# Attention with a bias: one VectorE product over four score banks instead of two, E tiles of twelve banks, AV lag of four slots

## The chip, the cores and the metric

The kernel runs on one core of a Trainium2 chip. The metric is the device time of one execution in microseconds (us), as a median over runs. The profiles give a "span", which is about 2 us shorter than the time of the same run. All runs compared here are of the fast state; one early run of the kernel before took 303.93 us and is left out. Ratios are the mean time of one kernel's runs over that of the other's in the same rounds, so they are not quite the ratio of the medians quoted.

Engine names in the profile lines: PE is TensorE (PEld its weight loads), DVE is VectorE, ACT is ScalarE, POOL is GpSimd. "L120" is line 120 of that kernel's source; the same statement has another line number in another version, so lines are named by what they do.

## The reference

Inputs are q, k and v of shape 4 x 8 x 1024 x 64 (32 heads) and one bias of 1024 x 1024 shared by all heads.

```python
scores = scale * np.matmul(q, k.transpose(0, 1, 3, 2)) + bias
attn = np.exp(scores - max) / (sum of exp + 1e-8)
out = np.matmul(attn, v)
```

The kernel uses exp(s + bias) = exp(s) * exp(bias). It keeps exp(bias^T) in bf16 as `eb`, computes E = exp(scale * k q^T) on ScalarE and multiplies E by `eb` on VectorE. A column of ones appended to v makes the AV product ("attention times v") deliver the sums of the softmax too.

## The kernel before

The heads are taken in 16 pairs. A score bank is 128 keys x 512 queries, and the program walks through 512 of them. Each slot makes three banks on TensorE into one of only two score buffers and one exponential on ScalarE reads them:

```python
ps_s = ctx.enter_context(tc.tile_pool(name="ps_s", bufs=2, space=bass.MemoryType.PSUM))  # 2 x 3 banks
ps_x = ctx.enter_context(tc.tile_pool(name="ps_x", bufs=1, space=bass.MemoryType.PSUM))  # tags xa, xb: 1 bank each
...
def s_slot(g):
    ps = ps_s.tile([P, 3, HQ], F32, tag="s", name="ps")
    ...  # three matmuls, kT x qT
    nc.scalar.activation(e[:, o:o + n, :], ps[:, :n, :], ACTF.Exp, scale=scale)

def mul_pair(b):                       # VectorE, two banks (both heads of a key chunk share eb)
    ...
    nc.vector.tensor_tensor(e[:, o:o + 2, :], e[:, o:o + 2, :],
                            eb[:, qh, kc, :].unsqueeze(1).to_broadcast([P, 2, HQ]), op=ALU.mult)
```

Two uses share the bank "xa": the AV accumulator `po` of the first head, and the result `px` of transposing the next q or k. VectorE must empty either before TensorE may write the other:

```python
def transpose_pe(pr, which):
    px = ps_x.tile([P, NCH, P], BF, tag="xb" if pr < 2 and which else "xa", name="px")
    ...  # 16 transposes on TensorE
    def copy():                        # VectorE: masked copy to qT (q) or plain copy to kT (k)
        ...
    return copy

def av_bank(b):
    if kc == 0:
        po[h] = ps_x.tile([P, QC, D1], F32, tag="xa" if h == 0 else "xb", name="po")
    ...  # 4 matmuls; after the eighth bank it returns evac(), VectorE's normalisation
```

Each step of the main loop puts one slot in program order. In the traces VectorE's instructions come in that order, and one that waits holds up those behind it (below, a copy starts at 64.95 us behind a product that waited until 64.34):

```python
for step, item in enumerate(order):
    ...  # scores and exponential of this slot; in 28 steps a transpose of q or k
    ...  # up to four AV banks whose product is at least LAG = 3 steps old
    muls(1)              # a product of two banks, of exponentials up to the slot before
    for f in late:       # the copy of a transpose, and evacuations
        f()
    muls(2)
    exp_b = new_b
```

The softmax here doesn't subtract the row's maximum and nothing guards it: scores larger than these inputs give would overflow.

## Time and profile before

The median before is 266.6 us (11 runs, 265.5 to 267.5).

| reading | value | view |
|---|---|---|
| ScalarE busy | 91% of the span | page, busy times |
| VectorE, TensorE busy | 86%, 84% | page, busy times |
| pitch of exponentials, back to back | about 1.35 us | ScalarE's timeline |
| stops of ScalarE from 52 us to the end | 5.8 us in 13 stops | ScalarE's timeline |
| last exponential's end to the end of the span | 6.4 us | ScalarE's timeline |

Busy times of the page (us, share of the span, instructions), and two of its groups: the exponential, and the product. A group's columns are busy time and mean ns of one, then the engine's idle time before them and what ended most of it.

```profile
PE 221.0 (84%) x3136; PEld 137.6 (52%) x3136; DVE 227.2 (86%) x422; ACT 240.7 (91%) x179; POOL 52.5 (20%) x72
...
L120 ACT ACTIVATE E<-ps 128x1536 bf16<-128x1536 f32 x171 | 232.4, 1475 | 16.7 <-PE ps L113 14.6
L136 DVE TENSOR_TENSOR E<-E,eb 128x1024 bf16<-128x1024 bf16 x256 | 167.1, 687 | 18.9 <-ACT E L120 14.1
```

ScalarE is nearly full. VectorE waits for it directly; ScalarE waits for VectorE only through TensorE, as shown below. One exponential lasts 1.475 us, but the next starts before it ends, which is why the pitch is shorter. The Trainium skill ("ScalarE: Activation LUTs", What ACT_TABLE_LOAD costs) gives 186 ns plus 0.833 ns an element for an activation with immediate scale and bias, as here (the kernel gives a number for the scale and no bias). That makes an estimate of 1466 ns; the trace agrees (1475 ns).

ScalarE's own timeline (start, length, what, count; in brackets the idle time before) shows how little room is left:

```profile
51.98 15.01 ACT L120 ACTIVATE E<-ps 128x1536 bf16<-128x1536 f32 x11 [0.32 <-PE ps L113]
67.48 14.88 ACT L120 ACTIVATE E<-ps 128x1536 bf16<-128x1536 f32 x11 [0.48 <-ACT E L120]
82.92 13.60 ACT L120 ACTIVATE E<-ps 128x1536 bf16<-128x1536 f32 x10 [0.56 <-PE ps L113]
96.84 15.02 ACT L120 ACTIVATE E<-ps 128x1536 bf16<-128x1536 f32 x11 [0.32 <-PE ps L113]
```

Three stops return every 44.86 us, in which three head pairs (32 slots) pass. The Trainium skill ("Perfetto Trace Analysis", Optimization Strategy) says that a gap that repeats on the engine that should be saturated can mean too little SBUF or PSUM for the next tile. Here it fits in part: the stop of 0.48 us comes from the single bank "xa". The timeline of that stop, with weight loads left out:

```profile
62.85 4.14 ACT L120 ACTIVATE E<-ps 128x1536 bf16<-128x1536 f32 x3
...
63.76 0.64 PE L86 MATMUL px<-ident,qr 128*64 128x128 bf16 x16
...
64.34 0.69 DVE L136 TENSOR_TENSOR E<-E,eb 128x1024 bf16<-128x1024 bf16 x1 [0.24 <-ACT E L120]
64.46 0.81 PE L113 MATMUL ps<-qT,kT 128*128 128x512 bf16 x3
64.95 1.22 DVE L92 TENSOR_TENSOR qT<-px,mask 128x2048 bf16<-128x2048 bf16 x1
...
66.22 0.53 PE L150 MATMUL po<-vall,E 128*128 128x65 bf16 x12 [0.83 <-DVE qT L92]
66.58 0.81 PE L113 MATMUL ps<-qT,kT 128*128 128x512 bf16 x3
...
67.48 1.45 ACT L120 ACTIVATE E<-ps 128x1536 bf16<-128x1536 f32 x1 [0.48 <-ACT E L120]
```

Read it as a chain. TensorE transposes q into "xa". VectorE has a product before the copy in its order; the product waits for an exponential until 64.34, and so the copy qT runs from 64.95 to 66.17. TensorE needs "xa" for AV, stands 0.83 us, and makes the next scores only at 66.58. ScalarE starts at 67.48 instead of 67.00. The two score buffers hide only a part of such a stand: in one period TensorE's stands behind q copies of 0.71, 0.83 and 0.95 us became stops of 0.32, 0.48 and 0.56 us, and its stands behind k copies (0.42, 0.30 and 0.17 us) became none. About 0.4 us is hidden. The bracket of this last line names ScalarE itself as the releaser; it is put down to the last event that the profile saw, and the scores that end just before are the better reading.

Who waited for whom over the whole run (us in total, times, longest):

```profile
PE po L150 <- DVE qT L92: 10.9, 14, 1.0
...
PE po L150 <- DVE kT L97: 4.3, 14, 0.4
```

### The profile page before, as it was taken

Reading aid. Unit: us, or ns where it says so; the run is one execution under the profiler, and the core shown is the slowest. Engines: PE = TensorE matmul, PEld = TensorE weight load, DVE = VectorE, ACT = ScalarE, POOL = GpSimd, SP = SyncE. Lnnn points to the kernel's source line nnn. Section 1 sums busy time; section 2 is a strip of 40 time slices with the busy share of each in tenths; the row PEclk is TensorE's granted clock in tenths of the full one; section 3 lists DMA queues with packets and bytes.
Section 4 is the critical chain, followed back from the end, with each engine's and each line's share of the span. In section 5 each row is a group of like instructions: output and inputs, shape, how many; then the busy total and the mean of one; then the engine's idle time right before and its main releaser. Section 6 shows DMA issues by size and latency. Waiting matters only on the chain.

```text
span 264.5 us, 7204 instructions
## 1 busy us (share of the span) xinstructions
PE 221.0 (84%) x3136; PEld 137.6 (52%) x3136; DVE 227.2 (86%) x422; ACT 240.7 (91%) x179; POOL 52.5 (20%) x72
## 2 busy tenths in 40 slices
PE   1577879888998989899898989899898989899883
PEld 1244545555655555555555555555555555555552
DVE  4246679998999999899899899989999998998984
ACT  2289999999999999999999999999999999999990
POOL 8353004022130404031040404022091000000000
PEclk9999999999999999999999999999999999999999
DMA  6999904919191673929194684919089201111112
GB/s 89 176 217 185 170 1 94 108 46 157 43 148 14 119 81 77 126 51 151 40 122 43 106 94 98 102 42 161 17 150 118 82 0 42 42 40 42 40 43 79
DMA packets 46912, 23.53 MB, mean 89 GB/s; under 512 B 34337, under 2 KB 42529, under 8 KB 46625
## 3 DMA queue, kind: packets, MB, share of 16 engines
q0 software_dynamic: 42272, 14.68, 51.8%
q1 hardware_dynamic: 4608, 8.39, 8.7%
q8 instruction: 24, 0.39, 0.6%
q14 instruction: 8, 0.06, 0.1%
HBM read 29.36 MB, written 8.39 MB: 143 GB/s over the span
## 4 chain that ended last, share of the span: by engine, by line
ACT 44%; DVE 26%; PE 18%; DMA 4%; issue 4%; POOL 2%; ACTq 0%; POOLq 0%
ACT E L120 42%; DVE E L136 16%; PE ps L113 13%; DVE qT L92 5%; PE po L150 5%; DMA qr<-in_q_dram 4%; DVE kT L97 3%; ACT eb L130 2%; DVE oall L161 2%; DVE rs L160 1%; POOL vall L76 1%; POOL kr L70 1%; ACTq L120 0%; POOL qr L71 0%; PE px L86 0%
## 5 line engine op out<-in xcount | busy, mean ns | idle before, releaser
L120 ACT ACTIVATE E<-ps 128x1536 bf16<-128x1536 f32 x171 | 232.4, 1475 | 16.7 <-PE ps L113 14.6
L136 DVE TENSOR_TENSOR E<-E,eb 128x1024 bf16<-128x1024 bf16 x256 | 167.1, 687 | 18.9 <-ACT E L120 14.1
L113 PE MATMUL ps<-qT,kT 128*128 128x512 bf16 x512 | 139.7, 382 | 14.5 <-ACT E L120 10.9
L150 PEld LDWEIGHTS <-E 128*128 128x128 bf16 x2048 | 84.2, 98 | 54.6 <-issue 19.5
L150 PE MATMUL po<-vall,E 128*128 128x65 bf16 x2048 | 94.1, 194 | 16.1 <-DVE qT L92 10.9
L113 PEld LDWEIGHTS <-kT 128*128 128x128 bf16 x512 | 44.2, 98 | 45.1 <-issue 20.7
L70 POOL DMA_DIRECT2D kr<-in_k_dram x16 | 11.3, 708 | 139.7 <-PE px L86 86.0
L161 DVE TENSOR_TENSOR oall<-po,rs 128x256 f32<-128x256 f32 x64 | 27.2, 425 | 2.2
L76 POOL DMA_DIRECT2D vall<-in_v_dram x32 | 28.1, 883 | 0.0
L92 DVE TENSOR_TENSOR qT<-px,mask 128x2048 bf16<-128x2048 bf16 x16 | 19.5, 1219 | 2.5 <-PE px L86 2.3
L97 DVE COPY kT<-px 128x1024 bf16<-128x1024 bf16 x16 | 11.0, 685 | 7.5 <-PE px L86 7.5
L86 PE MATMUL px<-ident,kr 128*64 128x128 bf16 x256 | 10.6, 228 | 5.8 <-DMA kr<-in_k_dram 5.8
L86 PEld LDWEIGHTS <-kr 128*64 128x64 bf16 x256 | 8.0, 113 | 11.8 <-issue 5.9
L71 POOL DMA_DIRECT2D qr<-in_q_dram x16 | 11.7, 729 | 6.2 <-PE ps L113 5.6
L86 PE MATMUL px<-ident,qr 128*64 128x128 bf16 x256 | 10.6, 228 | 2.0 <-DMA qr<-in_q_dram 2.0
L86 PEld LDWEIGHTS <-qr 128*64 128x64 bf16 x256 | 8.0, 113 | 8.3 <-DMA qr<-in_q_dram 5.4
L160 DVE RECIPROCAL rs<-po 128x4 f32<-128x4 f32 x64 | 11.2, 175 | 1.0 <-PE po L150 1.0
L130 ACT ACTIVATE eb<-pb 128x1536 bf16<-128x1536 bf16 (+1 forms) x6 | 7.9, 1321 | 0.0
L126 PEld LDWEIGHTS <-btraw 128*128 128x128 bf16 x64 | 4.9, 147 | 3.3 <-issue 2.4
L126 PE MATMUL pb<-ident,btraw 128*128 128x128 bf16 x64 | 4.9, 225 | 1.5 <-ACT eb L130 1.2
L182 DVE MEMSET mask<- 64x1024 bf16 (+1 forms) x4 | 2.8, 698 | 0.5 <-issue 0.2
L175 ACT ACT_TABLE_LOAD x1 | 1.3, 1283 | 0.7 <-PEq L289 0.7
(11 smaller groups left out, 2.6 us busy)
## 6 DMA issues: line engine op xcount, KB each, us to landing
out_dram<-oall SPq DMA_DIRECT2D x32, 256.0 KB, 2.0
kr<-in_k_dram POOLq DMA_DIRECT2D x16, 256.0 KB, 4.0
qr<-in_q_dram POOLq DMA_DIRECT2D x16, 256.0 KB, 5.6
vall<-in_v_dram POOLq DMA_DIRECT2D x32, 128.0 KB, 6.5
btraw<-in_bias_dram POOLq DMA_DIRECT2D x2, 1024.0 KB, 13.3
```

The source lines that it names most:

```text
L70: nc.gpsimd.dma_start(out=kr.rearrange("p t c d -> p t (c d)"), in_=kf[pr])
L76: nc.gpsimd.dma_start(out=vall[:, 2 * pr + t, :, :D], in_=vf[pr, :, t])
L86: nc.tensor.transpose(px[t * D:(t + 1) * D, c, :], src[:, t, c, :], ident[:])
L92: nc.vector.tensor_tensor(dst[:], px.rearrange("p c q -> p (c q)").unsqueeze(1).to_broadcast([P, 2, NCH * P]), mask[:], op=ALU.mult)
L97: nc.vector.tensor_copy(dst[:], px[:])
L113: nc.tensor.matmul(ps[:, j, :], kT[:, kc, :], qT[:, h, qh * HQ:(qh + 1) * HQ], start=True, stop=True)
L120: nc.scalar.activation(e[:, o:o + n, :], ps[:, :n, :], ACTF.Exp, scale=scale)
L130: nc.scalar.activation(eb[:, qh, kcs[0]:kcs[0] + n, :], ps[:, :n, :HQ], ACTF.Exp)
L136: nc.vector.tensor_tensor(e[:, o:o + 2, :], e[:, o:o + 2, :], eb[:, qh, kc, :].unsqueeze(1).to_broadcast([P, 2, HQ]), op=ALU.mult)
L150: nc.tensor.matmul(acc[:, i, :], e[:, b % 6, i * P:(i + 1) * P], vall[:, 2 * pr + h, kc, :], start=(kc == 0 and i == 0), stop=(kc == NCH - ...
L160: nc.vector.reciprocal(rs[:], acc[:, :, D:D1])
L161: nc.vector.tensor_tensor(oall[:, qh * QC:(qh + 1) * QC, :], acc[:, :, :D], rs[:].to_broadcast([P, QC, D]), op=ALU.mult)
```

## The change

The intent: VectorE pays its fixed part once for four banks instead of once for two, with 127 instructions fewer. Tiles of twelve banks let a group of four never cross a tile, and the longer lag gives AV the time that the coarser products take. The core of the diff, with cuts marked:

```diff
-    ep = ctx.enter_context(tc.tile_pool(name="ep", bufs=12))      # tiles of 6 banks
+    ep = ctx.enter_context(tc.tile_pool(name="ep", bufs=6))       # tiles of ET = 12 banks
...
+    def mul_pair(b, n=4):
...
+        e = e_at(b, n)
+        if n == 4:
+            e = e.rearrange("p (c t) q -> p c t q", t=2)
+            nc.vector.tensor_tensor(e, e, eb[:, qh, kc:kc + 2, :].unsqueeze(2).to_broadcast([P, 2, 2, HQ]),
+                                    op=ALU.mult)
...
-        LAG = 3
+        LAG = 4
...
-            while n and mul_next + 2 <= exp_b:
+            while n and mul_next < NB:
...
+                w = 4 if mul_next < NB - 4 else 2
+                if mul_next + w > exp_b or (qh, kc + w // 2 - (w > 1)) not in eb_have:
+                    break
...
             muls(1)
             for f in late:
                 f()
-            muls(2)
+            muls(1)
```

A product of four banks now may start only when the exponentials of all four are there, and a copy still stands behind one product in each step that has one ready.

More of the change, by code (lines that the diff above doesn't have):

```diff
@@ L103, with e_at @@
     NB = len(banks)
-    slots = [banks[i:i + 3] for i in range(0, NB, 3)]
+    slots = [list(range(i, min(i + 3, NB))) for i in range(0, NB, 3)]
     NS = len(slots)
+    ET = 12
     etiles = {}
+    def e_at(b, n):
+        b = b
+        if b // ET not in etiles:
+            etiles[b // ET] = ep.tile([P, ET, HQ], BF, name="E")
+        return etiles[b // ET][:, b % ET:b % ET + n, :]
     def s_slot(g):
@@ L110, in s_slot @@
         sl = slots[g]
-        for j, (pr, h, qh, kc) in enumerate(sl):
+        n = len(sl)
+        for j, b in enumerate(sl):
+            pr, h, qh, kc = banks[b]
             qT, kT = trs[(pr, 0)], trs[(pr, 1)]
@@ L114, in s_slot @@
                              start=True, stop=True)
-        if g % 2 == 0:
-            etiles[g // 2] = ep.tile([P, 6, HQ], BF, name="E")
-        e = etiles[g // 2]
-        o = 3 * (g % 2)
-        n = len(sl)
-        nc.scalar.activation(e[:, o:o + n, :], ps[:, :n, :], ACTF.Exp, scale=scale)
+        nc.scalar.activation(e_at(sl[0], n), ps[:, :n, :], ACTF.Exp, scale=scale)
     def b_slot(qh, kcs):
@@ L130, in b_slot @@
         nc.scalar.activation(eb[:, qh, kcs[0]:kcs[0] + n, :], ps[:, :n, :HQ], ACTF.Exp)
-    def mul_pair(b):
+    def mul_pair(b, n=4):
         pr, h, qh, kc = banks[b]
-        e = etiles[b // 6]
-        o = b % 6
-        nc.vector.tensor_tensor(e[:, o:o + 2, :], e[:, o:o + 2, :],
-                                eb[:, qh, kc, :].unsqueeze(1).to_broadcast([P, 2, HQ]),
-                                op=ALU.mult)
+        e = e_at(b, n)
[3 more added lines that the diff above has]
+                                    op=ALU.mult)
+        else:
+            nc.vector.tensor_tensor(e, e, eb[:, qh, kc:kc + 1, :].to_broadcast([P, n, HQ]),
+                                    op=ALU.mult)
     oalls = {}
@@ L147, in av_bank @@
         acc = po[h]
-        e = etiles[b // 6]
+        e = e_at(b, 1)
         for i in range(QC):
-            nc.tensor.matmul(acc[:, i, :], e[:, b % 6, i * P:(i + 1) * P], vall[:, 2 * pr + h, kc, :],
+            nc.tensor.matmul(acc[:, i, :], e[:, 0, i * P:(i + 1) * P], vall[:, 2 * pr + h, kc, :],
                              start=(kc == 0 and i == 0), stop=(kc == NCH - 1), skip_group_check=True)
@@ L205 @@
             pend_t += [(pr, 0, (pr - 2) * 32 + 8), (pr, 1, (pr - 2) * 32 + 24)]
-        gap = None
-        LAG = 3
+        LAG = 4
         def muls(n):
             nonlocal mul_next
-            while n and mul_next + 2 <= exp_b:
+            while n and mul_next < NB:
                 pr, h, qh, kc = banks[mul_next]
-                if (qh, kc) not in eb_have:
+                w = 4 if mul_next < NB - 4 else 2
+                if mul_next + w > exp_b or (qh, kc + w // 2 - (w > 1)) not in eb_have:
                     break
-                mul_pair(mul_next)
-                mul_done[mul_next] = mul_done[mul_next + 1] = step
-                mul_next += 2
+                mul_pair(mul_next, w)
+                for b in range(mul_next, mul_next + w):
+                    mul_done[b] = step
+                mul_next += w
                 n -= 1
@@ L221 @@
         for step, item in enumerate(order):
-            prev_b = exp_b
             if item[0] == "S":
@@ L225 @@
                 s_slot(g)
-                new_b = min(NB, 3 * (g + 1))
+                new_b = slots[g][-1] + 1
             else:
```

## The prediction

> **What bounds it now.** ScalarE. In its timeline the exponentials of 1536 columns run back to back about 1.35 us apart (11 in 15.01 us); 171 of them and six of the bias (7.9 us) fill nearly all of the time from 11.7 to 258 us. VectorE (86% busy on the page) is not the limit: it idles 14.1 us waiting for the exponential (table of waits). From 52 us on, ScalarE stops in one place only: 0.32, 0.48, 0.56 us, repeating every 44.86 us (32 slots, three head pairs), 13 stops, 5.8 us in all. Each follows a transpose of q: TensorE runs into an AV bank that needs the accumulator bank "xa", which VectorE still empties (masked copy qT, 1.22 us), and stands (10.9 us over 14 waits for qT); the next scores come late, and only two score buffers lie between. So: product 64.34, qT 64.95 to 66.17, TensorE resumes 66.22, scores 66.58, ScalarE starts 67.48 instead of 67.00. The copies of kT (0.68 us) make TensorE wait 0.3 us each, which costs ScalarE nothing.
>
> **What the change removes.** 256 products of 687 ns become 126 of 2048 elements and two of the old size. The Trainium skill ("VectorE: DVE Perf Modes", side-by-side cycles) gives about 150 cycles fixed plus half a cycle an element; the trace's pair fits (687 ns against 690), so a four-bank product should take about 1.22 us and run at a pitch of 1.15 to 1.17. Products: 167 us busy down to about 148; VectorE near 208. That lies off the critical path.
>
> **What it moves.** On VectorE a four-bank product, waiting for the latest exponential, now often stands before the q or k copy where a pair stood. From the order of instructions (period of three head pairs), with t = 0 the end of that exponential:
> - q after such a product (pairs of heads 3, 6, ...): qT ends at 0.06+1.15+1.22 = 2.43, TensorE resumes, three AV banks 0.36, scores to ScalarE 0.90: 3.74 against 2.72 due; stop 1.0 us (was 0.32).
> - next pair: the q copy has no product in its step: about 0.1 (was 0.48).
> - third pair: product behind an evacuation and two others, about 0.2 late: 1.2 (was 0.56).
> - k copies: two in three now behind a four-bank product, about 0.65 and 0.45 (was 0); the third 0.
>
> Sum over the head pairs: 5x1.65 + 4x0.55 + 4x1.2 = 15 us of stops against 5.8: +9 us in theory; I shade it to +8. The longer lag leaves 22 instead of 17 AV banks after the loop, but most run under the last exponentials, and the last evacuation of the odd head comes earlier: -0.3 to +0.8 us. Start unchanged.
>
> **Predicted:** 274.5 us, range 266 to 281. Faster by over 2%: 0.04; within 2%: 0.31; slower by over 2%: 0.65.
>
> **What would show it.** Four-bank products at 1.2 us; VectorE's share down to about 75 to 80%; ScalarE's exponential still about 1.35 us pitch; in its timeline stops of about 1 us after q transposes and of half a microsecond after k transposes; waits of TensorE's AV for qT and kT growing from 15.2 us to about 25; period of three head pairs about 47 us instead of 44.86.
>
> **What would make it wrong.** If the product lost its two-per-cycle rate with the four-dimensional pattern (2.2 us each, VectorE the limit: above 290 us; unlikely, the innermost 512 stay contiguous). If exponentials run ahead or VectorE drains its queue earlier than I reckon, so that the product before the copy is already done: then stops stay as they are, and the time falls within 1%. At best the 5.8 us of stops are won: 261.

## The result, and the profile after

The changed kernel takes 275.8 us (median of 4, 275.3 to 277.6), against 266.6: a ratio of 1.037 (interval 1.032 to 1.042). It is slower by 9.2 us.

The page's busy times and the same two groups:

```profile
PE 221.0 (80%) x3084; PEld 139.5 (51%) x3136; DVE 214.4 (78%) x295; ACT 240.8 (87%) x179; POOL 52.7 (19%) x72
...
L124 ACT ACTIVATE E<-ps 128x1536 bf16<-128x1536 f32 x171 | 232.3, 1476 | 26.3 <-PE ps L122 25.2
L141 DVE TENSOR_TENSOR E<-E,eb 128x2048 bf16<-128x2048 bf16 x127 | 153.2, 1220 | 42.1 <-ACT E L124 39.9
```

The intent was met: 127 long products of 1.22 us, and VectorE is busy for 12.8 us less. (The prediction said 126 long and two short products; there are 127 and two.) ScalarE's work is the same to 0.1 us; its idle time grew. VectorE's saving went into waiting: for the exponential alone it waits 39.9 us instead of 14.1.

ScalarE's timeline over one period:

```profile
102.51 8.16 ACT L124 ACTIVATE E<-ps 128x1536 bf16<-128x1536 f32 x6 [0.97 <-PE ps L122]
111.24 13.61 ACT L124 ACTIVATE E<-ps 128x1536 bf16<-128x1536 f32 x10 [0.57 <-PE ps L122]
125.29 8.16 ACT L124 ACTIVATE E<-ps 128x1536 bf16<-128x1536 f32 x6 [0.43 <-PE ps L122]
134.56 13.54 ACT L124 ACTIVATE E<-ps 128x1536 bf16<-128x1536 f32 x10 [1.10 <-PE ps L122]
149.06 8.16 ACT L124 ACTIVATE E<-ps 128x1536 bf16<-128x1536 f32 x6 [0.97 <-PE ps L122]
```

Four stops in a period of 46.55 us, 3.07 us together instead of 1.36. The stop of 0.97 us in detail, weight loads left out:

```profile
98.30 0.64 PE L86 MATMUL px<-ident,qr 128*64 128x128 bf16 x16
...
98.88 1.22 DVE L141 TENSOR_TENSOR E<-E,eb 128x2048 bf16<-128x2048 bf16 x1 [0.78 <-ACT E L124]
99.00 0.81 PE L122 MATMUL ps<-qT,kT 128*128 128x512 bf16 x3
...
100.03 1.22 DVE L92 TENSOR_TENSOR qT<-px,mask 128x2048 bf16<-128x2048 bf16 x1
...
101.30 0.53 PE L157 MATMUL po<-vall,E 128*128 128x65 bf16 x12 [1.36 <-DVE qT L92]
101.66 0.81 PE L122 MATMUL ps<-qT,kT 128*128 128x512 bf16 x3
...
102.51 1.45 ACT L124 ACTIVATE E<-ps 128x1536 bf16<-128x1536 f32 x1 [0.97 <-PE ps L122]
```

It is the same chain with a longer link (the stop of the same place in the period was 0.32 us before). VectorE was idle for 0.78 us because the four-bank product had to wait for its last bank; the transposed q was nearly ready, and the copy stood behind. Again about 0.4 us of a stand is hidden: the stands of 1.36, 0.96, 0.83 and 1.50 us from 53 to 87 us became stops of 1.02, 0.57, 0.44 and 1.10 us, and one of 0.36 us became none. TensorE's waits for the two copies grew from 15.2 us to 22.4:

```profile
PE po L157 <- DVE qT L92: 14.3, 13, 1.5
...
PE po L157 <- DVE kT L97: 8.1, 9, 1.0
```

At the end there is a second loss. The evacuation that frees "xa" for the even head's second query half stands behind a four-bank product that waits for an exponential, and TensorE stands for 1.33 us:

```profile
267.15 1.23 DVE L141 TENSOR_TENSOR E<-E,eb 128x2048 bf16<-128x2048 bf16 x1 [1.33 <-ACT E L124]
268.30 0.18 DVE L167 RECIPROCAL rs<-po 128x4 f32<-128x4 f32 x1
268.51 0.42 DVE L168 TENSOR_TENSOR oall<-po,rs 128x256 f32<-128x256 f32 x1
...
268.99 1.04 PE L157 MATMUL po<-vall,E 128*128 128x65 bf16 x28 [1.33 <-DVE oall L168]
```

From the last exponential's end to the end of the span it is 7.5 us (the last exponentials run from 250.90 for 17.14 us, so to 268.04; the span ends at 275.5) instead of 6.4. How much of this is the evacuation is taken up below. The sum: the stops from 52 us on (here from 54 us) are 13.9 us instead of 5.8, which is 8.1 us, and the end adds 1.05. As a check, from the start of ScalarE's long run of scores (33.33 and 31.27 us) to the end of the span the two profiles differ by 8.9 us, of the 9.2 by which the medians differ. The profiled run of the changed kernel lost about 2 us more before 33 us; its granted TensorE clock was 0.7 in two slices there (mean 0.988), and it is the slowest of the kernel's runs (277.6). Runs with a clock of 0.996 or 1.00 took 275.3 to 275.8, so that part is not counted as the change's. That the clock caused it is not shown: the other runs left no trace.

### The profile page after: what moved, and what is told of

Same layout as the page of the kernel before. It is cut to its first block, busy times and chain, and to the rows that moved or that the text cites. A ratio compares the mean times of both kernels' runs of the same rounds, so it can differ in the third digit from the quotient of the medians.

```text
span 275.5 us, 6993 instructions
## 1 busy us (share of the span) xinstructions
PE 221.0 (80%) x3084; PEld 139.5 (51%) x3136; DVE 214.4 (78%) x295; ACT 240.8 (87%) x179; POOL 52.7 (19%) x72
## 4 chain that ended last, share of the span: by engine, by line
ACT 54%; DVE 22%; PE 10%; issue 7%; DMA 4%; POOL 2%; POOLq 0%
ACT E L124 52%; DVE E L141 13%; PE ps L122 5%; DMA qr<-in_q_dram 4%; PE po L157 4%; DVE qT L92 4%; DVE kT L97 2%; ACT eb L134 2%; DVE oall L168 2%; DVE rs L167 1%; POOL vall L76 1%; POOL kr L70 1%; PE pb L130 0%; DVE E L144 0%; PE px L86 0%
## 5 line engine op out<-in xcount | busy, mean ns | idle before, releaser
L141 DVE TENSOR_TENSOR E<-E,eb 128x2048 bf16<-128x2048 bf16 x127 | 153.2, 1220 | 42.1 <-ACT E L124 39.9
L122 PE MATMUL ps<-qT,kT 128*128 128x512 bf16 x460 | 137.9, 385 | 17.3 <-ACT E L124 10.7
L157 PEld LDWEIGHTS <-E 128*128 128x128 bf16 x2048 | 83.1, 98 | 59.4 <-issue 25.1
L157 PE MATMUL po<-vall,E 128*128 128x65 bf16 x2048 | 92.8, 194 | 24.3 <-DVE qT L92 14.3
L122 PEld LDWEIGHTS <-kT 128*128 128x128 bf16 x512 | 45.1, 98 | 49.2 <-issue 20.0
L130 PEld LDWEIGHTS <-btraw 128*128 128x128 bf16 x64 | 5.8, 154 | 3.3 <-issue 3.1
L130 PE MATMUL pb<-ident,btraw 128*128 128x128 bf16 x64 | 5.9, 253 | 1.5 <-ACT eb L134 1.4
## 6 DMA issues: line engine op xcount, KB each, us to landing
btraw<-in_bias_dram POOLq DMA_DIRECT2D x2, 1024.0 KB, 13.3
```

The lines of the kernel that those rows point to most:

```text
L122: nc.tensor.matmul(ps[:, j, :], kT[:, kc, :], qT[:, h, qh * HQ:(qh + 1) * HQ], start=True, stop=True)
L141: nc.vector.tensor_tensor(e, e, eb[:, qh, kc:kc + 2, :].unsqueeze(2).to_broadcast([P, 2, 2, HQ]), op=ALU.mult)
L157: nc.tensor.matmul(acc[:, i, :], e[:, 0, i * P:(i + 1) * P], vall[:, 2 * pr + h, kc, :], start=(kc == 0 and i == 0), stop=(kc == NCH - 1), ...
```

## The experiments

The theory: work on VectorE that is ordered ahead of the copy holds the bank "xa"; TensorE, in order, stands before AV and brings the scores late; ScalarE stops. The rivals: the lag of four or the tiles starve an engine; or the long VectorE instruction disturbs the others by itself. Eleven kernels were run; each computed the right result.

### The copy ahead of the product, in the changed kernel and in the kernel before

```diff
+                early.append(transpose_pe(pr, which))     # was: late.append
...
+            for f in early:
+                f()
             muls(1)
             for f in late:
                 f()
```

> The changed kernel with one thing moved: in the 28 slots that transpose q or k, VectorE makes the copy before the product instead of after it. Theory (a four-bank product ahead of the copy holds the accumulator bank, TensorE stands, ScalarE stops): the recurring stops of the exponential, 3.07 us in each period of three head pairs, shrink to under 0.5 us, the period falls from 46.55 us to about 43.6, and the time to 262 to 263.5 us, below the kernel before. Rival (lag of four or the tiles of twelve banks starve TensorE or ScalarE): the stops stay and the time is 272 us or more. Second rival (longer VectorE instructions slow ScalarE or TensorE themselves): also 272 or more.

> The kernel before with the copy moved ahead of the product. Theory: its three stops of 0.32, 0.48 and 0.56 us in each period go, 5.8 us in all: 260 to 261.5 us, unless VectorE, 95% busy in these stretches, becomes the limit, which would leave 262 to 265 us. Rival (copies have nothing to do with the stops): 266.5 us.

Measured: the changed kernel with this one move 261.7 us (ratio to before 0.979, interval 0.973 to 0.986); the kernel before with it 259.7 us (0.974, 0.969 to 0.979). ScalarE's timeline after the start is a single line in each, first the changed kernel, then the kernel before:

```profile
32.20 219.41 ACT L124 ACTIVATE E<-ps 128x1536 bf16<-128x1536 f32 x163
```

```profile
31.41 219.72 ACT L120 ACTIVATE E<-ps 128x1536 bf16<-128x1536 f32 x163
```

TensorE's waits for the q copy, from the two tables of waits, again first the changed kernel; no stand is longer than the 0.4 us that is hidden:

```profile
PE po L157 <- DVE qT L92: 4.5, 13, 0.4
```

```profile
PE po L150 <- DVE qT L92: 4.2, 14, 0.4
```

163 exponentials without one stop, 1.35 us apart. Long products, tiles and lag are all still there in the first of the two, so none of them costs ScalarE anything once the copy does not stand behind a product. The move took 14.1 us off the changed kernel and 6.9 us off the kernel before, somewhat more than their stops (13.9 and 5.8), and both times lie just below the expected ranges. A stop costs more than its bracket: the exponential after it lasts 1.45 us and has no overlap with the one before, where the pitch is 1.35. So the 163 exponentials took 226.82 us in the kernel before (31.27 to 258.09) against 219.72 here, which is 7.1 us for 13 stops of 5.8, about 0.1 us more for each. The changed kernel with the move is still 2.0 us slower than the other; in the two profiles its end is longer (8.1 against 6.4 us) and its start 0.8 us later. The rivals predicted no change. VectorE, busy for 41.80 us of a period's 44.86 before the move (93%), did not become the limit in the kernel before either.

### Two pair products in the place of each long one

The edit, abridged:

```diff
-            nc.vector.tensor_tensor(e, e, eb[...].to_broadcast([P, 2, 2, HQ]), op=ALU.mult)
+            for i in range(2):
+                nc.vector.tensor_tensor(e[:, 2*i:2*i+2, :], e[:, 2*i:2*i+2, :], eb[...], op=ALU.mult)
```

> The changed kernel with each four-bank product issued as two products of two banks in the same place, so order, tiles and lag are the change's and the instruction's length is the old one. Theory (what counts is how much product work stands ahead of the copy): two pairs take about 1.28 us where one four-bank product took 1.15, so the stops grow from 3.07 us in a period to 3.5 to 4.5, and the time is 277 to 281 us. Rival (the long instruction itself does harm): back to 266 to 269 us.

Measured: 270.1 us (ratio to before 1.013, 1.008 to 1.017). Both expectations missed. A period has stops of 0.48, 0.50 and 1.04 us, 2.02 us instead of 3.07. The timeline of the 0.48 us stop, which is the changed kernel's 0.97:

```profile
95.00 0.68 DVE L141 TENSOR_TENSOR E<-E,eb 128x1024 bf16<-128x1024 bf16 x1
...
95.93 0.69 DVE L141 TENSOR_TENSOR E<-E,eb 128x1024 bf16<-128x1024 bf16 x1 [0.24 <-ACT E L124]
...
96.53 1.22 DVE L92 TENSOR_TENSOR qT<-px,mask 128x2048 bf16<-128x2048 bf16 x1
...
97.81 0.53 PE L158 MATMUL po<-vall,E 128*128 128x65 bf16 x12 [0.83 <-DVE qT L92]
...
99.06 1.45 ACT L124 ACTIVATE E<-ps 128x1536 bf16<-128x1536 f32 x1 [0.48 <-ACT E L124]
```

The expectation had put both pairs after the latest exponential. The first pair needs only banks that are there a slot earlier, and it runs in time in which the long product could only wait; only the second, 0.6 us, lies between the exponential and the copy. In this stop and in the one of 0.43 us, which is gone, the last four banks straddle two exponentials in that way. In the other two all the pairs need the latest exponential: there nothing was won (0.50 for 0.57, 1.04 for 1.10). So the harm of the long product is not only its length. It waits for the last of its four banks with all of its work still to do. That joining accounts for 5.7 of the 9.2 us (275.8 to 270.1).

### The lag alone, taken away and added

```diff
-        LAG = 4
+        LAG = 3     # in the changed kernel; the reverse in the kernel before
```

> The changed kernel with the AV lag back at three slots. Theory: the lag only shifts in which slots a four-bank product falls together with a copy; the stops are of the same sizes in another sequence, their sum within 1.5 us over the kernel, and fewer AV banks are left after the loop: 273.5 to 276 us. Rival (the lag costs the time): 269 us or less.

> The kernel before with the AV lag of four slots, pairs and tiles unchanged. Theory: the lag by itself only moves the slots in which q and k are transposed; stops of ScalarE of about 1.2 to 1.6 us in a period of three head pairs against 1.36, one to five AV banks more after the loop: 266 to 268 us. Rival (the lag is the cause of the loss): 271 us or more.

Measured: the changed kernel with a lag of three 274.4 us (1.027 of before, 1.021 to 1.034), with the same four sizes of stops (0.97, 0.57, 0.43, 1.10) in another sequence: as expected. The kernel before with a lag of four 269.2 us (1.012, 1.008 to 1.017), which is 1.2 us above the expected range. Its stops are 0.49, 0.56 and 0.61 us instead of 0.32, 0.48 and 0.56; over the run 7.3 us instead of 5.8. Its end is 6.9 us instead of 6.4, and its uninterrupted stretches are about 0.2 us longer in a period. The lag is therefore not free: it costs about 3 us with pairs. With the long products the medians differ by 1.4 us, but the intervals overlap and the stops of the two profiles by only 0.6 (13.9 and 13.3), so that part may be noise. By the program order the longer lag moves the transposes into slots with other products ahead of the copy.

### The tiles of twelve banks alone

The changed source with `w = 2`, `muls(2)` after the copies and `LAG = 3`.

> The changed source set back to pairs, two pairs after the copies, and a lag of three: what is left of the change is the E tiles of twelve banks, six of them. Theory: the tiles cost nothing: 266 to 267.2 us, three stops of 0.32, 0.48 and 0.56 us in a period as before. Rival (tiles that are freed twelve banks at a time hold up ScalarE): 270 us or more, with stops of the exponential that end with TensorE's AV.

Measured: 266.1 us against 266.0 (0.9997, 0.996 to 1.004), stops of 0.31, 0.43 and 0.56 us. The tiles cost nothing.

### More work ahead of the copy, in the kernel before

```diff
-            muls(1)
+            muls(2)
             for f in late:
                 f()
-            muls(2)
+            muls(1)
```

> The kernel before with up to two pair products ahead of the copies and one after, instead of one ahead and two after: more product work in front of the copy, with no long instruction, no new tiles and no new lag. Theory (work in front of the copy makes the stop): stops grow from 1.36 to about 2.0 to 2.6 us a period, 269 to 273 us. Rival (the order does not matter, something else in the change does): 266.5 us.

Measured: 271.7 us (1.020, 1.017 to 1.024). A period of ScalarE's timeline:

```profile
68.45 14.88 ACT L120 ACTIVATE E<-ps 128x1536 bf16<-128x1536 f32 x11 [1.09 <-issue]
83.89 6.82 ACT L120 ACTIVATE E<-ps 128x1536 bf16<-128x1536 f32 x5 [0.56 <-PE ps L113]
91.26 6.82 ACT L120 ACTIVATE E<-ps 128x1536 bf16<-128x1536 f32 x5 [0.55 <-ACT E L120]
98.40 15.02 ACT L120 ACTIVATE E<-ps 128x1536 bf16<-128x1536 f32 x11 [0.32 <-PE ps L113]
```

The stops are 2.5 us together instead of 1.36. Nothing of the change is in this kernel, only a second pair ahead of the copy, and more than half of the loss is there.

### All copies and evacuations first

`for f in early + late: f()` ahead of both products: in the kernel before, and in the changed kernel.

> The kernel before with copies and evacuations both ahead of the products of their slot. Theory: no stops in the middle, as with the copy alone, and an equal or shorter end: 259 to 260 us, equal within noise to the copy-first kernel's 259.7. If evacuations that wait for AV hold up the products behind them, AV waits for products and it is 261 or more.

> The changed kernel with copies and evacuations ahead of the product in every slot. It differs from the changed kernel with only the copies first in the place of the evacuations. Theory: at the end, TensorE no longer stands 1.34 us for an evacuation that waits behind a four-bank product, so from the last exponential's end to the end of the span it is about 6.3 us instead of 7.5 to 8, and the time is 260 to 261 us. If that wait is not on the path at the end: 261.7 as with the copies alone.

Measured: with pairs 259.2 us (0.973, 0.969 to 0.977), with long products 260.7 us (0.978, 0.975 to 0.980). No stops in either. With the long products the end shrank from 8.1 us (copies first only) to 7.0, not to 6.3: the 1.33 us stand is gone, but AV now waits for products (0.39, 0.27 and 0.23 us). About 0.6 of the 8.1 was slower AV in that one profile, 1.75 us for 32 matmuls instead of 1.16, at a clock of 0.6 in its last slice. So about half a microsecond was won at the end.

### Two versions for the best time

As above, and the transposes of the second head pair at step 5 instead of 3, with pairs; the same with long products and a lag of three.

> The kernel before with copies and evacuations ahead of the products, and the transposes of the second head pair two slots later (at step 5 instead of step 3), so that TensorE does not stand before their loads while ScalarE waits for scores (1.3 us of ScalarE in the trace of before, near 18 us). Theory: 257.5 to 258.7 us, about 1 us under the pairs with all copies first (259.2). If the loads only make it stand later: 259.2.

> The same two moves in the changed kernel, with its lag back at three slots: four-bank products, copies and evacuations first, transposes of the second head pair at step 5. Theory: once no product stands ahead of a copy, ScalarE sets the pace with either product, VectorE's relief is worth nothing: 257.5 to 259.5 us, within 1 us of the version with pairs. If the relief of VectorE is worth something there: 1.5 us or more below it.

Measured, five rounds each: 258.8 us with pairs (0.972, 0.969 to 0.974), 258.8 us with long products (0.970, 0.968 to 0.973). Both beat both kernels, by 2.9% and 6.2% of the medians. The later transposes brought nothing that can be told from noise: 258.8 is just above the expected range, the wait of 1.3 us near 18 us is gone, but in both profiles ScalarE waits for a bias transpose near 24 us (1.8 and 1.9 us) and its uninterrupted part starts at 32.0 and 32.1 us, as without the move. Pairs and long products end equal. With nothing in front of the copies, VectorE's relief is worth nothing, because ScalarE sets the pace.

## Why the prediction was right

**The limit.** Right. ScalarE's pitch was the same before and after (43.47 and 43.48 us of work in a period), and freed of its stops it ran 163 exponentials in a row.

**What the change removes.** Right, a little too large. The long product takes 1.220 us (the estimate of 1.22 was worked out from the fixed part and half a cycle an element of the Trainium skill, "VectorE: DVE Perf Modes", side-by-side cycles; the trace agrees, and the two-per-cycle rate survived the four-dimensional pattern). Products take 153 us in place of the 148 predicted, because the pitch of 1.15 holds only back to back; 44 now start after a wait for the exponential, and others follow a copy or an evacuation. VectorE is busy for 214 us where 208 was predicted, 78% of the span where it was 75 to 80%. None of it came into the time.

**What it moves.** Right in each row:

| stop, us | before | predicted | after |
|---|---|---|---|
| q copy, head pairs 3, 6, ... | 0.32 | 1.0 | 0.97 |
| q copy, next pair | 0.48 | 0.1 | none seen |
| q copy, third pair | 0.56 | 1.2 | 1.10 |
| k copies | 0 | 0.65, 0.45, 0 | 0.57, 0.43, none |
| all from 52 us on | 5.8 | 15 | 13.9 |

The growth of 8.1 us is the "+8" of the prediction. The rows themselves gave +9; the shading to +8 has no reason beside it, so that it hit to 0.1 us is luck. Moving the copy took all of it away again. The waits for the copies grew to 22.4 us where 25 was expected, and the period to 46.55 us where 47 was.

**The end.** This step failed. "The last evacuation of the odd head comes earlier: -0.3 to +0.8 us" looked at the odd head; an evacuation of the even head (of its first query half) stands behind a long product, and the end grew by 1.05 us. That is the mechanism of the copies again, in a place where the prediction did not look, but it is not the whole: with the evacuation moved ahead about half a microsecond was won. The rest was not separated; the longer lag with pairs has an end of 6.9 us, and with the long products AV still waits for a product (0.39 us the longest).

**The lag.** The prediction let it matter only through the order. That holds, but the effect is not small: 3 us with pairs.

In all: 274.5 us were predicted and 275.8 measured, and the parts agree with the sum within 0.3 us: 7.9 from the stretch of the exponentials (the stops grew by 8.1) and 1.05 from the end. Going from one kernel to the other by steps: the tiles 266.1, the lag with pairs 269.2, two pairs in the place of the long product 270.1, the long product 275.8. The steps depend on each other and are not a sum of independent costs; the lag is worth at most 1.4 us at the other end.

## What to carry to other kernels

Before saving work on an engine that is not the limit, look at what stands behind that work in its order. A longer instruction that waits for more inputs delays everything behind it, here a short copy that held the only free accumulator bank, and the two score buffers hid only about 0.4 us of TensorE's stand. Put what releases a scarce buffer ahead of bulk work that has slack: that move was worth 2.6% by itself in the kernel before, where the larger products had cost 3.7%. Whether a second bank in the place of the shared "xa" would do the same was not tried.

## What the Trainium skill lacked or had wrong

- "VectorE: DVE Perf Modes", tier table: it puts `tensor_tensor` with any PSUM operand at one element per cycle. The masked copy qT, a `tensor_tensor` of 2048 bf16 elements (1024 from PSUM, each used twice, and 2048 from SBUF), took 1.219 us, the same as 2048 elements from SBUF alone (1.220 us), which is the two-per-cycle time. The text under the table allows two per cycle for 16-bit PSUM operands, so the column should say so.
- "ScalarE: Activation LUTs", What ACT_TABLE_LOAD costs: back-to-back instructions overlap by about 93 ns there. Here the exponential of 1536 columns lasts 1475 ns at a pitch of about 1346 ns (163 in 219.41 us), an overlap of about 130 ns.
- "Perfetto Trace Analysis", Optimization Strategy: it lists buffer count and tile sizes as causes of repeating gaps (and says before that, in general, to make the blocking dependency start sooner). The order of instructions on the engine that frees the buffer belongs beside them: with the same buffers, moving the copy ahead of one product took out 13 stops of 5.8 us.
- No page says that joining instructions makes the joined one wait for the last of its inputs. Here that was worth 5.7 us of the 9.2 (275.8 us joined, 270.1 us as two in the same place).
